# The gate z stored without its SiLU, squares summed by VectorE, and a norm placed between blocks of the first output product

## The chip, the cores and the metric

The kernel runs on one core of a Trainium2 chip. The metric is the time of one execution on the device in microseconds; the median of a few runs is compared. A profile shows one execution, instruction by instruction, on TensorE (PE, with its weight loads as PEld), VectorE (DVE), ScalarE (ACT), GpSimd (POOL) and SyncE (SP), whose queue issues most of the DMAs.

## The reference, cut to what matters

One layer of a decoder trunk with two parallel groups of heads, over 1056 tokens (1024 of a prompt, 32 of samples), width 1024:

```python
n = rmsnorm(h, g_in); z_a, xbc, dt_raw, z_b, u_b = split(n @ w_in)
# group A: SSD scan y over chunks of 128 tokens, then, in 2 groups of 512 channels,
y = y * silu(z_a)
ya = y * rsqrt(mean(y * y, -1) + EPS) * ssd_norm_g
# group B: S5 scan y, then the GLU
g = gelu(y)
yb = g * sigmoid(g @ glu_w + glu_b) * silu(z_b)
h = h + concat(ya, yb) @ w_out          # then a gate with a second norm, and the final norm
```

## The kernel before

All matrices are kept with channels on the 128 partitions and tokens along the free axis, in 8 tiles of 128 channels. Each product is made from three matmuls per step, since weights and operands are split into a high and a low part (`split`: ScalarE makes the high part, VectorE the low one). `dense` makes one output tile of 128 channels in three chunks of tokens, 24 matmuls to a chunk, into one of the three PSUM buffers `psd`, and calls `evac` for each chunk. Weights come through `take_w`, which loads and splits one tile ahead.

The order is planned: the program is written in one sequence, and a planner puts each engine's instructions in an order by a model of their times; an engine then runs its list strictly in that order, and so does the queue of SP. `behind(ins)` and `issue_after` force an instruction after another on the same engine.

The stages follow one another as here, in us of the profiled execution:

1. 0 to 210: the norm of the input, the tiles of u, and three tiles of `z_b`.
2. 210 to 476: convolution tiles, and between them 16 batches of the S5 scan (`s5_batch`, whose tables `mm`, `om`, `u8` are loaded into two buffers each, and which ends in the matmuls `yp`), sums of output weights (`wo_sums`), and five more tiles of `z_b`.
3. 476 to 657: 16 units of the SSD scan (`ssd_first`, `ssd_second`), eight tiles of `z_a` between them (by `z_tile`, as for `z_b`), and towards the end `g_tile`, which loads the S5 result and splits it for the GLU.
4. 657 to 742: the GLU. For each of 8 tiles m: 72 matmuls, and for each chunk of it the load of z_b (tile `gzl`), Tanh of the product (`zt`), the load of g (`gg`) and two scalar_tensor_tensor operations into `yb`; then `za_apply(m)`, which loads z_a (`zl`), multiplies it into `xs[m]`, squares the result and sums the squares of four tiles into `ysq`. All these small tiles share one pool `ev` of six buffers.
5. 742 to 912: the output product, seven block products `PROD` of eight blocks (24 matmuls each) with operands `opn` made by `operand`. `ya_norm(g)` normalizes a group of four tiles of `xs`: `rstd_tok` sums `ysq` over channels with 12 narrow matmuls into `nsp` and takes the root in small VectorE operations, `rstd_bcast` spreads it over partitions with 12 matmuls into `nrb`, and 12 scalar_tensor_tensor operations apply it. It is written for group 0 after tile 3 of the GLU and for group 1 after the GLU.
6. 912 to 1027: the gate, and the last norm.

In `z_evac` each chunk of z is made into 2·silu(z) before it is stored: ScalarE writes Tanh(z/2) and VectorE adds one and multiplies by z, from PSUM. The factors 0.25 and `4 * EPS` further on take the doubling back.

The profile names operations by the line of a helper: L77 is any ScalarE activation (`act`), L80 add, subtract and multiply, L92 scalar_tensor_tensor, L233 and L247 the matmuls of `dense` and `dense_k`, L1221 those of the output product, L274 and L296 those of the norm sums and their spreading, L309 and L312 those of the S5 batch. On SP's queue L743 and L754 store z, L767 loads `zl`, L1157 loads `gzl`, and L791 loads `mm`.

Of the kernel before, what the change touches and what calls it, by code (L numbers as in the profile page):

```python
# [10 lines left out]
AF = mybir.ActivationFunctionType  # L11
# [13 lines left out]
CW = 352  # L25
# [15 lines left out]
def hymba_ssd_s5_kernel(  # L41
# [216 lines left out]
    def rstd_tok(chunks, n, eps=EPS, after=None, pause=None):  # L258
# [6 lines left out]
        for c, sqs in enumerate(chunks):  # L265

            for i, q in enumerate(sqs):
# [4 lines left out]
                for j in range(gr):  # L272
# [4 lines left out]
                    if after is not None:  # L277
                        after = pe_end[0] = end
        v, y, t = (nw_p.tile([128, 16], F32, tag=q, name=q, bufs=b)[0:qt, 0:w]
                   for q, b in (("nv", 2), ("ny", 3), ("nt", 2)))  # L280
        ts(v, sp[0:qt, 0:w], 1.0 / n, eps, ALU.mult, ALU.add)
# [453 lines left out]
    def z_evac(j):  # L735
        dst = zb_d[j] if j < 8 else za_d[j - 8]

        def evac(c, t0, n, ps):
            t = ev("zt", n)
            if j >= 8:  # L740
                act(t, ps, AF.Tanh, scale=0.5)
                v_mid[0] = stt(t, t, 1.0, ps, ALU.add, ALU.mult)
                dma(out=dst[:, t0:t0 + n], in_=t)  # L743
                return

            nn = min(n, NPT - t0)
            for a, b, d0, ns in ((0, nn, 0, 8),) + (((nn, n, NPT, 4),) if nn < n else ()):
                v = t[:, a:b].rearrange("p (s c) -> p s c", s=ns)
                pv = ps[:, a:b].rearrange("p (c s) -> p s c", s=ns)
                act(v, pv, AF.Tanh, scale=0.5)  # L750
                v_mid[0] = stt(v, v, 1.0, pv, ALU.add, ALU.mult)
# [11 lines left out]
    def za_apply(j):  # L763
        for c in range(3):
            t0 = CW * c
            t = ev("zl")
            dma(out=t, in_=za_d[j, :, t0:t0 + CW])  # L767
            y = xs[j][:, t0:t0 + CW]
# [6 lines left out]
            else:  # L775
                act(t, y, AF.Square)
                add(ysq[c], ysq[c], t, G)
# [214 lines left out]

    def ya_norm(g):

        rt = rstd_tok([[ysq[c]] for c in range(3)], 512, 4 * EPS)
        for c in range(3):
            rs = rstd_bcast(rt[:, 4 * c:4 * c + 4])
            for i in range(4):
                y = xs[4 * g + i][:, CW * c:CW * c + CW]
                stt(y, y, vc[:, V_NG + 4 * g + i:V_NG + 4 * g + i + 1], rs, ALU.mult, ALU.mult)  # L1000
# [15 lines left out]
    k = 3  # L1016
# [134 lines left out]
    for m in range(8):  # L1151
# [3 lines left out]
        def evac(c, t0, n, ps):  # L1155
            z = ev("gzl", n)
            dma(out=z, in_=zb_d[m, :, t0:t0 + n])  # L1157
            t = ev("zt", n)
# [9 lines left out]
            for yv, a, b, s, s0 in ((y[:, 0:NPT], 0, nn, 8, t0 // 128),) + (((y[:, NPT:T], nn, n, 4, 0),) if nn < n else ()):  # L1168
                zv, tv = (r[:, a:b].rearrange("p (s c) -> p s c", c=128 if s == 8 else 8) for r in (z, t))
                stt(yv.rearrange("p (c s) -> p s c", s=s)[:, s0:s0 + zv.shape[1]], zv, 0.25, tv, ALU.mult, ALU.mult)  # L1170
# [14 lines left out]
    def banks():  # L1185
        return [f("psd")[:, 0:CQ] for f in (lambda n: psd_(), lambda n: psd_(), lambda n: psd_(), psa, psa, psb, psb, psb)]
# [253 lines left out]
```

## Time and profile before

| | |
|---|---|
| median of three runs | 1028.26 us (1025.12 to 1031.12) |
| the profiled execution | 1028.4 us |
| its span, first to last instruction | 1026.6 us |
| what lies around the span | 1.8 us |
| granted TensorE clock, mean | 0.994 of full speed |
| busy shares | PE 97%, DVE 79%, ACT 44%, POOL 16% |

A busy share is an average over six stages with different limits; matmuls are pipelined, so that PE counts as busy while one matmul is being fed and another drains. What PE is short of is its idle time, 1026.6 - 996.4 = 30.2 us over the whole span. A row of a stretch gives the busy time of each engine in it with the number of its instructions. A row of waits gives who waited, for whom, the sum in us, how often, and the longest.

### The profile page before, as it was taken

How to read it: one execution, taken by the hardware profiler on the slowest of the kernel's cores; microseconds unless marked ns; L12 is line 12 of the kernel's file. 1: busy time of each engine (PE TensorE's matmuls, PEld its weight loads, DVE VectorE, ACT ScalarE, POOL GpSimd, SP SyncE). 2: the span in 40 equal slices, each digit the busy share in tenths (PEclk: the TensorE clock that was granted, in tenths of full speed). 3: DMA queues.
4: the chain of work that ended last, by engine and by line, in shares of the span. 5: the costliest groups of instructions: out<-in, count | busy, mean ns of one | idle time of the engine just before them, and what ended most of it. 6: DMA issues, size and time to landing. Idle time of an engine off the chain costs nothing.

```text
span 1026.6 us, 19644 instructions
## 1 busy us (share of the span) xinstructions
PE 996.4 (97%) x7214; PEld 945.3 (92%) x7214; DVE 809.5 (79%) x1880; ACT 454.6 (44%) x1009; POOL 164.9 (16%) x183
## 2 busy tenths in 40 slices
PE   9999999999999989999999997999999999999997
PEld 8999999979899989899887886899999999999996
DVE  5889989675998978984687768868778879986466
ACT  5733223345453434354865436344345435464221
POOL 0000000000000000002144233121232015641221
PEclk9999999999999989999999999999999999999999
DMA  9633489774658687755366668675634323335123
GB/s 315 219 77 120 148 254 245 198 244 132 196 168 255 193 236 206 207 155 183 113 185 200 204 189 224 170 201 166 176 114 136 112 90 125 120 114 171 50 95 106
DMA packets 181072, 174.89 MB, mean 170 GB/s; under 512 B 47728, under 2 KB 145520, under 8 KB 180976
## 3 DMA queue, kind: packets, MB, share of 16 engines
q1 hardware_dynamic: 150944, 153.23, 50.1%
q10 hardware_dynamic: 30032, 20.40, 6.4%
q8 instruction: 57, 0.93, 0.4%
q14 instruction: 39, 0.32, 0.1%
HBM read 123.05 MB, written 54.73 MB: 173 GB/s over the span
## 4 chain that ended last, share of the span: by engine, by line
PE 54%; DVE 8%; DMA 6%; issue 4%; ACT 2%; SPq 1%; POOL 0%; POOLq 0%; DVEq 0%; ACTq 0%
PE psd L233 30%; PE psd L1221 15%; DMA mm<-md 2%; PE yp L312 2%; ACT ab L77 1%; DMA ab<-acs_d 1%; PE nrb L296 1%; PE yd L873 1%; DVE acc L92 1%; PE yo L922 1%; DMA gr<-gd 1%; PE st L925 1%; DVE x L92 1%; DVE sst L80 1%; PE nsp L274 1%
## 5 line engine op out<-in xcount | busy, mean ns | idle before, releaser
L233 PE MATMUL psd<-n_h,wl 128*128 128x352 f32 x840 | 274.3, 327 | 1.4 <-DVE wl L80 1.4
L233 PE MATMUL psd<-n_h,wh 128*128 128x352 f32 x840 | 274.8, 327 | 0.0
L233 PE MATMUL psd<-n_l,wh 128*128 128x352 f32 x840 | 274.5, 327 | 0.0
L1221 PE MATMUL psd<-opn,wh 128*128 128x264 f32 x896 | 164.6, 285 | 1.7 <-DVE opn L80 1.7
L233 PEld LDWEIGHTS psd<-n_h,wh 128*128 128x128 f32 x840 | 158.7, 189 | 6.4 <-issue 6.1
L233 PEld LDWEIGHTS psd<-n_h,wl 128*128 128x128 f32 x840 | 158.7, 189 | 5.6 <-issue 3.4
L233 PEld LDWEIGHTS psd<-n_l,wh 128*128 128x128 f32 x840 | 158.7, 189 | 3.2 <-issue 2.9
L1221 PEld LDWEIGHTS psd<-opn,wh 128*128 128x128 f32 x896 | 138.8, 188 | 2.1 <-DVE opn L80 2.1
L80 DVE TENSOR_TENSOR wl<-wr,wh 128x512 fp32r<-128x512 f32 x146 | 106.3, 755 | 39.4 <-ACT wh L77 34.1
L77 ACT ACTIVATE wh<-wr 128x512 fp32r<-128x512 f32 x147 | 85.4, 622 | 105.5 <-PE psd L233 64.9
L1221 PE MATMUL psd<-opn,wl 128*128 128x264 f32 x448 | 127.1, 284 | 0.0
L1221 PEld LDWEIGHTS psd<-opn,wl 128*128 128x128 f32 x448 | 84.3, 188 | 0.0
L77 ACT ACTIVATE ab<-ab,tok 128x128 f32<-128x128 f32 (+1 forms) x144 | 42.9, 379 | 51.7 <-DMA ab<-acs_d 37.0
L233 PE MATMUL psd<-g_h,wh 128*128 128x384 f32 (+1 forms) x168 | 54.4, 324 | 0.0
L233 PE MATMUL psd<-g_l,wh 128*128 128x384 f32 (+1 forms) x168 | 54.0, 321 | 0.0
L233 PE MATMUL psd<-g_h,wl 128*128 128x384 f32 (+1 forms) x168 | 53.9, 321 | 0.0
L233 PE MATMUL psd<-hg_h,gwh 128*128 128x400 f32 (+1 forms) x144 | 46.7, 324 | 0.0
L233 PE MATMUL psd<-hg_l,gwh 128*128 128x400 f32 (+1 forms) x144 | 46.4, 322 | 0.0
L233 PE MATMUL psd<-hg_h,gwl 128*128 128x400 f32 (+1 forms) x144 | 46.3, 322 | 0.0
L77 ACT ACT_TABLE_LOAD x27 | 34.6, 1283 | 25.0 <-DVE acc L92 12.6
L92 DVE SCALAR_TENSOR_TENSOR zt<-zt,psd 128x352 f32<-128x352 f32 (+2 forms) x56 | 25.9, 463 | 23.3 <-ACT zt L77 23.0
L80 POOL TENSOR_TENSOR xl<-xl,h 128x264 f32<-128x264 f32 x32 | 29.8, 936 | 84.1 <-DMA xl<-xT 34.9
(323 smaller groups left out, 2044.3 us busy)
## 6 DMA issues: line engine op xcount, KB each, us to landing
wr<-wall SPq DMA_DIRECT2D x128, 256.0 KB, 3.4
mm<-md SPq DMA_DIRECT2D x16, 512.0 KB, 5.9
wa<-wall SPq DMA_DIRECT2D x32, 256.0 KB, 4.5
ws_d<-wa SPq DMA_DIRECT2D x16, 512.0 KB, 5.1
ab<-acs_d SPq DMA_DIRECT2D x16, 512.0 KB, 5.0
wr<-ws_d SPq DMA_DIRECT2D x32, 256.0 KB, 2.8
ud<-ub ACTq DMA_DIRECT2D x8, 576.0 KB, 4.8
u<-ud SPq DMA_DIRECT2D x16, 288.0 KB, 5.0
```

The lines of the kernel that those rows point to most:

```text
L77: return S.activation(out=out, in_=in_, func=func, **kw)
L80: return (eng or V).tensor_tensor(out=out, in0=a, in1=b, op=op)
L92: return V.scalar_tensor_tensor(out=out, in0=a, scalar=s, in1=b, op0=op0, op1=op1)
L233: end = PE.matmul(out=ps, lhsT=a[:, ko + k, :], rhs=b, start=(i == 0), stop=(i == 3 * K - 1))
L274: end = PE.matmul(out=sp[0:qt, gr * c + j:gr * c + j + 1], lhsT=q[:, qt * j:qt * j + qt], rhs=ones[:, 0:1], start=(i == 0 and j == 0), sto ...
L296: end = PE.matmul(out=rb[:, qt * j:qt * j + qt], lhsT=y[:, j:j + 1].to_broadcast([qt, 128]), rhs=ident[0:qt, 0:qt], start=True, stop=True)
L312: self.last = f(*a, **kw)
L873: PE.matmul(out=yd[64 * (e % 2):64 * (e % 2) + 64, e // 2], lhsT=x1[:, e], rhs=mt[:, e], start=True, stop=True)
L922: PE.matmul(out=yo[:, i], lhsT=hg[:, 128 * i:128 * i + 128], rhs=ct[g][:, cols], start=True, stop=True)
L925: PE.matmul(out=st, lhsT=bk, rhs=x2.rearrange("p e q -> p (e q)"), start=True, stop=True)
L1221: PE.matmul(out=ps, lhsT=a[:, k, :], rhs=b, start=(k == 0 and q == 0), stop=(k == 7 and q == 2))
```

## The change

1. `z_evac` stores z itself: ScalarE copies each chunk from PSUM to `zt`, and VectorE has no part in it any more (56 scalar_tensor_tensor operations fall away). `v_mid`, the mark behind which `wo_sums` is forced, is then set by the convolution alone.
2. In the GLU stage ScalarE applies Silu to `gzl` (24 chunks) and to `zl` (24 chunks) in place, before they are used; the factor 0.25 becomes 0.5 and `4 * EPS` becomes `EPS`.
3. The sums into `ysq` (18 adds) go from GpSimd to VectorE.
4. `ya_norm(0)` moves from the end of GLU tile 3 to tile 4, ahead of `za_apply(4)`. The operands of the first block product are made in the other order: those of yb at tile 4, those of xs at tile 5. Those of the second block product likewise begin with yb.
5. `ya_norm(1)` is cut into pieces that stand between blocks of the first block product, and the matmuls of blocks 0 to 5 and of the pieces are forced into one order: after each of the blocks 0, 1 and 2 the four sums of one chunk, after block 2 the root, after block 4 the spreading and the 12 operations that apply it. Each block takes its PSUM buffer when it comes to it, and not all eight at the start.

```diff
             if j >= 8:
-                act(t, ps, AF.Tanh, scale=0.5)
-                v_mid[0] = stt(t, t, 1.0, ps, ALU.add, ALU.mult)
+                act(t, ps)
                 dma(out=dst[:, t0:t0 + n], in_=t)
...
-                act(v, pv, AF.Tanh, scale=0.5)
-                v_mid[0] = stt(v, v, 1.0, pv, ALU.add, ALU.mult)
+                act(v, ps[:, a:b].rearrange("p (c s) -> p s c", s=ns))
...
             dma(out=t, in_=za_d[j, :, t0:t0 + CW])
+            act(t, t, AF.Silu)
...
-                add(ysq[c], ysq[c], t, G)
+                add(ysq[c], ysq[c], t)
...
+    def ya_scale(g, c, rt):
+        rs = rstd_bcast(rt[:, 4 * c:4 * c + 4], pe_end[0])
+        for i in range(4):
+            y = xs[4 * g + i][:, CW * c:CW * c + CW]
+            stt(y, y, vc[:, V_NG + 4 * g + i:V_NG + 4 * g + i + 1], rs, ALU.mult, ALU.mult)
+
     def ya_norm(g):
-
-        rt = rstd_tok([[ysq[c]] for c in range(3)], 512, 4 * EPS)
+        pe_end[0] = None
+        rt = rstd_tok([[ysq[c]] for c in range(3)], 512)
         for c in range(3):
-            rs = rstd_bcast(rt[:, 4 * c:4 * c + 4])
...
+            ya_scale(g, c, rt)
...
             dma(out=z, in_=zb_d[m, :, t0:t0 + n])
+            act(z, z, AF.Silu)
...
+        if m == 4:
+            ya_norm(0)
         za_apply(m)
-        if m == 3:
-            ya_norm(0)
-        if m in (4, 5):
-            opn += operand("b11", range(4 * (m - 4), 4 * (m - 4) + 4))
-
-
-    ya_norm(1)
+        if m == 4:
+            opn = operand("b11", range(4, 8))
+        if m == 5:
+            opn = operand("b11", range(4)) + opn
...
+    def ya_piece(n):
+        if n < 3:
+            if n == 0:
+                ya1["sp"] = psa("nsp")
+            for j in range(4):
+                with behind(pe_end[0]):
+                    pe_end[0] = PE.matmul(out=ya1["sp"][0:88, 4 * n + j:4 * n + j + 1],
+                                          lhsT=ysq[n][:, 88 * j:88 * j + 88], rhs=ones[:, 0:1],
+                                          start=(j == 0), stop=(j == 3))
+        if n == 2:
+            ya1["rt"] = rstd_root(ya1["sp"][0:88, 0:12], 512)
+        if n == 4:
+            for c in range(3):
+                ya_scale(1, c, ya1["rt"])
...
-        bk = banks()
...
-                ps = bk[2 * i + c]
+                ps = bank(2 * i + c)
...
-                        PE.matmul(out=ps, lhsT=a[:, k, :], rhs=b, start=(k == 0 and q == 0),
-                                  stop=(k == 7 and q == 2))
+                        with behind(pe_end[0] if j == 0 and 0 < 2 * i + c < 6 else None):
+                            end = PE.matmul(out=ps, lhsT=a[:, k, :], rhs=b, start=(k == 0 and q == 0),
+                                            stop=(k == 7 and q == 2))
+                        if j == 0 and 2 * i + c < 6:
+                            pe_end[0] = end
+                if j == 0 and 2 * i + c < 5:
+                    ya_piece(2 * i + c)
...
-                    nxt += operand(PROD[j + 1][1], range(2 * i, 2 * i + 2))
+                    nxt += operand(PROD[j + 1][1], [(2 * i + q + (4 if j == 0 else 0)) % 8 for q in range(2)])
...
-        opn = nxt
+        opn = nxt[4:] + nxt[:4] if j == 0 else nxt
```

## Rows read from the trace of the kernel before

**Rows 1.** The page, part 1: busy time of each engine, share, instructions.

```profile
PE 996.4 (97%) x7214; PEld 945.3 (92%) x7214; DVE 809.5 (79%) x1880; ACT 454.6 (44%) x1009; POOL 164.9 (16%) x183
```

**Rows 2.** Stretches: length, busy us of each engine, clock, DMA share, GB/s.

```profile
657.40:742.30 84.90, 84.90 (x554) 84.90 (x553) 63.70 (x128) 31.99 (x65) 15.59 (x15) 1.00 0.66 187
...
617.00:657.00 40.00, 33.19 (x232) 26.52 (x230) 37.33 (x70) 20.46 (x46) 13.54 (x9) 0.96 0.72 196
210.00:476.00 266.00, 256.48 (x1872) 240.05 (x1871) 217.54 (x558) 118.84 (x257) 1.22 (x2) 0.99 0.67 197
```

**Rows 3.** What PE waited for, 210 to 476 us.

```profile
PE vi L309 <- DMA mm<-md: 6.5, 4, 2.9
PE vi L309 <- DVE tb L80: 1.2, 1, 1.2
```

**Rows 4.** The page, part 5: the group of z's VectorE operation.

```profile
L92 DVE SCALAR_TENSOR_TENSOR zt<-zt,psd 128x352 f32<-128x352 f32 (+2 forms) x56 | 25.9, 463 | 23.3 <-ACT zt L77 23.0
```

**Rows 5.** The chain that ended last, 252 to 276 us: start, us, what.

```profile
253.18 0.52 DVE zt L92
...
258.58 0.40 DVE zt L92
...
259.32 0.12 DVE zt L92
...
268.45 5.91 DMA mm<-md
...
274.40 0.33 PE vi L309
```

**Rows 6.** The same chain, 400 to 420 us.

```profile
415.44 0.43 DVE zt L92
```

**Rows 7.** What SP's queue waited for, whole span.

```profile
SPq L754 <- DVE zt L92: 32.8, 12, 12.9
...
SPq L743 <- DVE zt L92: 28.5, 10, 10.3
```

**Rows 8.** VectorE in order of time, at 617 us: start, us, operation, idle before.

```profile
617.10 0.52 DVE L92 SCALAR_TENSOR_TENSOR zt<-zt,psd 128x352 f32<-128x352 f32 x1 [4.48 <-ACT zt L77]
617.54 0.28 DVE L80 TENSOR_TENSOR yt<-yos,ee 128x128 f32<-128x128 f32 x1
...
619.30 0.73 DVE L92 SCALAR_TENSOR_TENSOR x<-x,dsk,yt 128x32 f32<-128x32 f32 x4
```

**Rows 9.** ScalarE in order of time: table loads, a Silu (128x1024) and a Tanh.

```profile
250.32 1.28 ACT L77 ACT_TABLE_LOAD   x1 [2.49 <-DMA acs_s<-dw]
251.62 1.18 ACT L77 ACTIVATE x<-acc 128x1024 f32<-128x1024 f32 x2
252.70 0.44 ACT L77 ACTIVATE zt<-psd 128x352 f32<-128x352 f32 x1
...
488.25 1.28 ACT L77 ACT_TABLE_LOAD   x1
```

**Rows 10.** Groups of the GLU stage, 657 to 742 us.

```profile
L92 DVE SCALAR_TENSOR_TENSOR yb<-gzl,gg 128x384 f32<-128x384 f32 (+2 forms) x29 | 18.7, 687 | 10.3 <-DMA gg<-gd 10.0
L80 POOL TENSOR_TENSOR ysq<-ysq,zl 128x352 f32<-128x352 f32 x15 | 15.6, 1063 | 68.0 <-ACT zl L77 68.0
...
L80 DVE TENSOR_TENSOR x<-zl,x 128x352 f32<-128x352 f32 x21 | 10.8, 544 | 3.0 <-DMA zl<-za_d 2.7
...
L77 ACT ACTIVATE zl<-x 128x352 f32<-128x352 f32 x15 | 7.3, 496 | 20.7 <-DVE x L80 19.8 <-DMA wr<-wall 0.8
```

**Rows 11.** The chain that ended last, 742 to 761 us.

```profile
742.34 7.69 PE psd L1221 x63
750.03 1.80 PE nsp L274 x24
751.83 5.60 PE psd L1221 x45
757.44 2.65 PE nrb L296 x24
```

**Rows 12.** SP's queue, GpSimd and VectorE in order of time, 742 to 765 us.

```profile
742.82 1.40 SPq L767 DMA_DIRECT2D zl<-za_d  x3
...
746.82 3.04 POOL L80 TENSOR_TENSOR ysq<-ysq,zl 128x352 f32<-128x352 f32 x3 [6.74 <-ACT zl L77]
...
758.34 5.99 DVE L92 SCALAR_TENSOR_TENSOR x<-x,vc,nrb 128x352 f32<-128x352 f32 x12 [0.43 <-PE nrb L296]
```

**Rows 13.** The tile zl: from issue to landing of its loads.

```profile
DMA to landing us min/median/max: 2.2/2.7/3.6
```

More of the change, by code (lines that the diff above doesn't have):

```diff
@@ L256, in rstd, with rstd_tok @@
         return rstd_bcast(rstd_tok([sqs], n))
-    def rstd_tok(chunks, n, eps=EPS, after=None, pause=None):
+    def rstd_tok(chunks, n, after=None, pause=None):
         sp = psa("nsp")
@@ L278, in rstd_tok, with rstd_root @@
                         after = pe_end[0] = end
+        return rstd_root(sp[0:qt, 0:w], n)
+    def rstd_root(sp, n):
+        qt, w = sp.shape
         v, y, t = (nw_p.tile([128, 16], F32, tag=q, name=q, bufs=b)[0:qt, 0:w]
                    for q, b in (("nv", 2), ("ny", 3), ("nt", 2)))
-        ts(v, sp[0:qt, 0:w], 1.0 / n, eps, ALU.mult, ALU.add)
+        ts(v, sp, 1.0 / n, EPS, ALU.mult, ALU.add)
         ts(y.bitcast(I32), v.bitcast(I32), 1, None, ALU.logical_shift_right)
@@ L748, in evac @@
                 v = t[:, a:b].rearrange("p (s c) -> p s c", s=ns)
-                pv = ps[:, a:b].rearrange("p (c s) -> p s c", s=ns)
-                act(v, pv, AF.Tanh, scale=0.5)
-                v_mid[0] = stt(v, v, 1.0, pv, ALU.add, ALU.mult)
+                act(v, ps[:, a:b].rearrange("p (c s) -> p s c", s=ns))
                 o = dst[:, 0:NPT] if d0 == 0 else dst[:, NPT:T]
@@ L990, in sample_end @@
             ssd_y(8, g, 32, yds[g], yo)
+    def ya_scale(g, c, rt):
[3 more added lines that the diff above has]
+            stt(y, y, vc[:, V_NG + 4 * g + i:V_NG + 4 * g + i + 1], rs, ALU.mult, ALU.mult)
     def ya_norm(g):
-        rt = rstd_tok([[ysq[c]] for c in range(3)], 512, 4 * EPS)
+        pe_end[0] = None
+        rt = rstd_tok([[ysq[c]] for c in range(3)], 512)
         for c in range(3):
-            rs = rstd_bcast(rt[:, 4 * c:4 * c + 4])
-            for i in range(4):
-                y = xs[4 * g + i][:, CW * c:CW * c + CW]
-                stt(y, y, vc[:, V_NG + 4 * g + i:V_NG + 4 * g + i + 1], rs, ALU.mult, ALU.mult)
+            ya_scale(g, c, rt)
     s5_es, sd_es = ExitStack(), ExitStack()
@@ L1169, in evac @@
                 zv, tv = (r[:, a:b].rearrange("p (s c) -> p s c", c=128 if s == 8 else 8) for r in (z, t))
-                stt(yv.rearrange("p (c s) -> p s c", s=s)[:, s0:s0 + zv.shape[1]], zv, 0.25, tv, ALU.mult, ALU.mult)
+                stt(yv.rearrange("p (c s) -> p s c", s=s)[:, s0:s0 + zv.shape[1]], zv, 0.5, tv, ALU.mult, ALU.mult)
         (dense_k if m == 0 else dense)(w, g_h, g_l, evac, chunks=PCH)
         yb.append(y)
+        if m == 4:
+            ya_norm(0)
         za_apply(m)
-        if m == 3:
-            ya_norm(0)
-        if m in (4, 5):
-            opn += operand("b11", range(4 * (m - 4), 4 * (m - 4) + 4))
-    ya_norm(1)
+        if m == 4:
+            opn = operand("b11", range(4, 8))
+        if m == 5:
+            opn = operand("b11", range(4)) + opn
     h_r = [row(f"h{m}") for m in range(8)]
@@ L1183, in hymba_ssd_s5_kernel, with bank @@
     hg_h, hg_l = [None] * 8, [None] * 8
-    def banks():
-        return [f("psd")[:, 0:CQ] for f in (lambda n: psd_(), lambda n: psd_(), lambda n: psd_(), psa, psa, psb, psb, psb)]
+    def bank(n):
+        return (psd_() if n < 3 else psa("psd") if n < 5 else psb("psd"))[:, 0:CQ]
+    ya1 = {}
+    def ya_piece(n):
[12 more added lines that the diff above has]
+                ya_scale(1, c, ya1["rt"])
     def hg_split(m):
```

## The prediction

> **What bounds the kernel now.** I read the page first, for the busy shares, then the busy times by stage, then what PE waited for in the stages with idle time, and only there the chain of waits back to its cause. The reader is to see in the page that PE is busy for 996.4 us [rows 1] of a span of 1026.6, so no change that leaves its matmuls as they are can win more than 30.2 us. In the stretches one sees where the idle time lies. In the GLU stage there is none: 84.90 busy of 84.90 [rows 2]. From 210 to 476 us it is 266.00 - 256.48 = 9.5 us, with VectorE busy for 217.54 (82%), and from 617 to 657 us it is 40.00 - 33.19 = 6.8 us, with VectorE busy for 37.33 of 40 [rows 2]. So the kernel is bound by PE, and VectorE is close behind it in two stretches, which are the only ones where freeing VectorE can matter. The rest of the idle time lies in the first 210 us and after the output product begins; nothing in the change reaches its causes there, and I count it as untouched.
>
> **The change part by part.** *VectorE's part in z goes.* 56 operations of 463 ns mean, 25.9 us in all, fall away [rows 4]; ScalarE's own operation stays, a copy in the place of a Tanh, over the same elements. Where VectorE is off the path that is worth nothing, and I look at the two stretches.
>
> From 210 to 476 us five tiles of z are made with four VectorE operations each, 20 × 0.463 = 9.3 us. PE's waits there that can hang on VectorE are five, 6.5 + 1.2 = 7.7 us, all at the first matmul of an S5 batch, four of them for the load of mm [rows 3]. I followed two back. Ahead of the load issued at 268.45 the chain passes through z's operation three times, 0.52 + 0.40 + 0.12 = 1.04 us [rows 5], since the store of a weight sum, and behind it in SP's queue the load of mm, waited for VectorE. Ahead of the one wait on VectorE itself it passes through 0.43 us [rows 6]. That is 1.47 us for two waits, and at that rate 3.7 us for five. The bounds: nothing, if planner or loads take the rest up, and 7.7 us, all the waits, since 9.3 us of VectorE's work goes. I take 3.7. What speaks for more is SP's queue: the stores of z stood in it waiting for VectorE for 32.8 + 28.5 = 61.3 us [rows 7], with loads queued behind them, and after the change they wait for ScalarE alone, some 0.5 us sooner each. I give that no price of its own, as most loads behind them are early enough; it is in the upper bound.
>
> From 617 to 657 us VectorE is nearly full. Just ahead of that, at 617.10, it stands idle for 4.48 us with z's operation at the head of its list, and that waits for ScalarE [rows 8]. Without it the operations behind it, on results that PE has already made (0.28 us and its like, and 0.73 us, 1.3 us together), can run in that gap, and z's own 0.43 us (from its start to that of the next) falls away there and once more at the last chunk of z: 1.3 + 2 × 0.43 = 2.2 us less in a stretch that VectorE fills [rows 8]. I take 2.0, a little off for the loads of the S5 result that share the path; bounds nothing and 6.8, the idle time there [rows 2].
>
> *Silu in the GLU stage.* 48 activations on 128x352 to 128x384. The trace has no Silu of that size; the nearest row is a Square of the same tile zl, 496 ns [rows 10]. So 48 × 0.50 = 24 us, on a ScalarE that is busy for 31.99 of 84.90 [rows 2]: 56 of 85, and PE hides it. The cover is PSUM: a chunk takes PE (84.9 - 4.5) / 21 = 3.8 us (norm matmuls taken off), and with three buffers its eviction may come two chunks, 7.7 us, late before PE waits. I take 0; the upper bound is in the rivals.
>
> Tanh and Silu alternate there, and a table load takes 1.28 us. The trace shows that it isn't needed between these two: after the load at 250.32 a Silu runs at 251.62 and a Tanh at 252.70 with none between [rows 9]. The last load stands at 488.25, for the exponentials of the SSD stage [rows 9]; so I expect one more load, or three if a Silu is planned between the last exponentials, 1.3 to 3.8 us on ScalarE, which is busy for 20.46 of 40 us there [rows 2]. I take 0.
>
> The Trainium skill (ScalarE: Activation LUTs, "Table sets: the hidden batching unit") says to batch activations by table set, and its list has Tanh with Exp and does not say where Silu is. By its "What ACT_TABLE_LOAD costs", 2.66 us for each switch with the drain, 48 switches would be an estimated 128 us. The trace has the same 1.28 us for the load, and no load between Silu and Tanh; so the rule stays a rival only.
>
> *Sums of squares.* 18 adds leave GpSimd, 15 of them in the stretch at 1063 ns, and come to VectorE at the 544 ns of a product of the same shape [rows 10]: 18 × 0.54 = 9.8 us on an engine busy for 63.70 of 84.90 [rows 2], thus 73.5 of 85. A buffer of `ev` is given back sooner, by 0.5 us for each add and by GpSimd's latency, which about pays for the Silu that holds it longer. Cost 0 while that cover stands.
>
> *Norm and operands moved.* Group 0's norm and the order of the operands move by one tile, three chunks of 3.8 us, within a stage where PE doesn't wait; the first product needs them a tile and a half later. Cost 0.
>
> *Group 1's norm between blocks.* PE's work is the same, 24 and 24 instructions, 1.80 and 2.65 us, and stands at nearly the same places: before, the sums came 7.69 us into the product and the spreading 15.1 us [rows 11]. What is new is that the order is forced and begins early. One block takes 24 × 7.69 / 63 = 2.93 us [rows 11], so the sums of chunk 0 stand at 742.34 + 2.93 = 745.3. The last z_a loads are issued from 742.82 [rows 12] and land 2.7 us later [rows 13], at 745.5; then Silu 0.50, product 0.54, Square 0.50, add 0.54: 747.6. PE waits 747.6 - 745.3 = 2.3 us, and all blocks of the product are queued behind it. Bounds: 0, if the loads get their buffers earlier than before; 4.6, if the sum is ready only when GpSimd's last was, at 746.82 + 3.04 = 749.9 [rows 12]. I take 2.3. Chunks 1 and 2 then have a block of time each. After block 4 three PSUM buffers hold the spread root, and block 5 needs the first of them: its four operations take 4 × 5.99 / 12 = 2.0 us [rows 12] after the first third of the spreading, 0.9 us, against the 2.65 us that PE spends on it [rows 11]: 0.3 us of wait, up to 1.6 if a weight split stands ahead on VectorE. I take 0.3. The second product's first operand needs nine of the twelve operations and a split, about 768 us, and PE comes to it at 742.34 + 8 × 2.93 + 4.45 + 2.6 = 772.8; nothing.
>
> **The sum.** -3.7 - 2.0 + 2.3 + 0.3 = -3.1 us. Against the profiled execution, 1028.4 (span 1026.6 and 1.8 around it), that is **1025.3 us**. The median of the runs, 1028.26, is the same within 0.2 us.
>
> **The rivals.** *All the stalls close.* The planner orders everything anew with 25.9 us less on VectorE; if the five waits go (7.7) and half the idle time at the end of the SSD stage (3.4), with no new wait in the product, it is 1028.4 - 11.1 = 1017.3 us. For it: VectorE is the releaser, direct or through SP, in the stalls that I followed. Against: four of the five end on a load.
>
> *Loads hide the gain.* If load time alone sets those waits, nothing is won, and the wait in the first product stays: 1028.4 + 2.6 = 1031.0 us. That is the case in which the change doesn't do what it removes work for.
>
> *The GLU falls behind (slower).* VectorE is idle there for 84.90 - 63.70 = 21.2 us, mostly waiting for loads into `ev` (10.0 for gg and 2.7 for zl among them [rows 10]). If these waits stayed as long as they are, with 9.8 us of adds on top and 0.50 us of Silu in the path of each of the 21 chunks, 10.5, VectorE would need 63.7 + 21.2 + 9.8 + 10.5 = 105.2 us for 84.9. PSUM hides 7.7, PE would wait 12.6: with the other terms 1025.3 + 12.6 = 1037.9 us. It decides from 84.9 + 7.7 - 73.5 = 19.1 us of waits on. For it: that is just less than the 21.2 of before. Against: a wait ends when its load lands, so adds before it shorten it, and buffers that GpSimd held are free sooner.
>
> *A table load at each change of function.* If Silu and Tanh needed tables of their own there, two loads in each of 24 chunks, 48 × 1.28 = 61.6 us, would bring ScalarE to 56 + 61.6 = 117.6 us in a stage of 84.9, 33 us more: 1058 us. That is the skill's batching rule at this kernel's own load time; the trace speaks against it [rows 9].
>
> **How the numbers follow.** Chances: the forecast 0.38, all stalls close 0.31, loads hide the gain 0.12, the GLU falls behind 0.15, table loads 0.04. 0.5% is about 5.1 us, which is about what a measurement here can tell from no change: below 1023.2 is faster, above 1033.5 slower. The forecast with the bounds of its terms runs from 1021 to 1029; I count 0.31 of it as the same and 0.07 as faster. So faster is 0.31 + 0.07 = 0.38, same 0.31 + 0.12 = 0.43, slower 0.19. The low end of the range, 1014, is where all the stalls close with the whole idle time of 617 to 657 (7.7 + 6.8 = 14.5 us off); the high end, 1036, takes in part of a GLU that falls behind and leaves the rest of it, and the table loads, out.
>
> **What the changed profile would show.** Right: no VectorE operation on zt before the GLU; PE's waits for mm down to about half of 6.5 us; PE still without idle time from the start to the end of the GLU, with ScalarE at some 56 of 85 us there and VectorE at some 73; one to three more table loads, none between Silu and Tanh; in the first product a wait of about 2 us at the first sums, on VectorE's add. Wrong: idle PE in the GLU at the first matmul of a chunk, waiting for Tanh, which itself waited behind a Silu for its load; or waits for mm as long as before. What would make the total wrong even if each part is right is the planner: with other times it may place S5 and SSD work otherwise, and the waits are set by that placing.

## The result, and the profile after

The changed kernel is slower: 1039.17 us median of 7 runs (1035.74 to 1044.55) beside 1029.17 for the kernel before (7 runs), a ratio of 1.010 with a 95% interval of 1.0071 to 1.013. The profiled execution took 1036.62 us, span 1034.8. The forecast was 1025.3 with a range to 1036, so even the high end was too low.

The page of the changed kernel, busy time of each engine and the group of table loads:

```profile
PE 995.8 (96%) x7214; PEld 944.9 (91%) x7214; DVE 794.9 (77%) x1842; ACT 480.2 (46%) x1062; POOL 147.8 (14%) x165
...
L77 ACT ACT_TABLE_LOAD x32 | 41.1, 1283 | 23.0 <-DVE acc L92 11.3
```

PE has the same 7214 matmuls and the same busy time as in [rows 1]; VectorE has 14.6 us less. PE's idle time grows from 30.2 to 39.0 us, which is more than the 8.2 us of the longer span. Where it lies, and where PE's matmuls run slower, is read from the stretches (length, busy us of PE, PEld, DVE, ACT, POOL, clock, DMA share, GB/s):

```profile
210.00:476.00 266.00, 260.20 (x1916) 243.12 (x1914) 212.47 (x541) 129.35 (x282) 5.04 (x14) 1.00 0.68 198
...
617.00:657.00 40.00, 35.04 (x230) 29.49 (x230) 38.79 (x66) 22.63 (x44) 11.18 (x9) 0.96 0.71 198
...
649.30:738.00 88.70, 87.24 (x547) 87.15 (x546) 64.63 (x135) 47.82 (x101) 0.00 (x0) 0.96 0.61 171
738.00:752.00 14.00, 4.91 (x39) 4.70 (x38) 10.61 (x21) 8.82 (x20) 1.21 (x1) 0.76 0.60 169
752.00:775.00 23.00, 22.55 (x179) 22.42 (x179) 13.60 (x33) 7.78 (x16) 4.37 (x6) 0.92 0.20 64
...
755.80:780.00 24.20, 23.75 (x202) 23.62 (x202) 16.48 (x37) 9.56 (x20) 6.53 (x5) 1.00 0.20 66
```

The first two answer to [rows 2]: PE is busy 3.7 us more from 210 to 476 us and 1.9 us more from 617 to 657. The GLU's tile 1 begins at 648.7 us instead of 656.8. But windows of fixed time no longer hold the same work (the planner has put PE's work in another order, and the last S5 matmul starts at 456.3 us instead of 475.2), and from 0 to 210 and 476 to 617 us PE is busy 1.6 and 2.0 us less. The same 4563 matmuls up to tile 1, before:

```profile
0.00:656.80 656.80, 635.59 (x4563) 585.86 (x4563) 528.43 (x1358) 302.50 (x719) 65.37 (x83) 0.99 0.65 193
```

and after:

```profile
0.00:648.70 648.70, 629.47 (x4563) 580.31 (x4563) 508.61 (x1302) 307.83 (x724) 63.59 (x83) 1.00 0.67 196
```

So PE's idle time up to tile 1 falls by only 2.0 us, from 21.2 to 19.2. The other 6.1 us of the 8.1 are the same matmuls in less busy time, with the granted clock at 1.00 instead of 0.99 on the mean.

Then the lead is lost. The GLU, which had PE busy for every microsecond at clock 1.00 [rows 2], has 1.5 us idle and a mean clock of 0.96. And from 738 to 752 us, at the head of the output product, PE works for 4.9 us of 14. From the first matmul of tile 1 to that of the product it is now 90.0 us (before 85.4), and the product's first eight blocks take 40.2 us (before 28.1): 8.1 us won, 4.6 + 12.1 = 16.7 lost.

What PE waited for in the changed kernel, longest group first (us in total, times, longest), and the place in order of time (start, us, operation, idle time before it):

```profile
PE nsp L1204 <- DVE ysq L80: 9.1, 1, 9.1
...
PE nsp L274 <- DVE ysq L80: 1.5, 1, 1.5
...
PE vi L313 <- DMA mm<-md: 0.7, 1, 0.7
```

```profile
741.47 0.28 PE L1246 MATMUL psd<-opn,wl 128*128 128x264 f32 x1
750.84 1.33 PE L1204 MATMUL nsp<-cs,ysq 128*88 128x1 f32 x8 [9.09 <-DVE ysq L80]
752.04 0.79 PE L1246 MATMUL psd<-opn,wh 128*128 128x264 f32 x2
752.63 0.42 PE L1246 MATMUL psd<-opn,wl 128*128 128x264 f32 x1
...
755.75 0.28 PE L1246 MATMUL psd<-opn,wl 128*128 128x264 f32 x1
```

One block is done, and PE stands 9.09 us at the first sums. Behind the wait a matmul of 128x264 takes 0.42 us instead of 0.28, until about 755.5.

In the GLU the 1.5 us of idle time are one wait too, at the sums of group 0:

```profile
697.82 1.33 PE L274 MATMUL nsp<-cs,ysq 128*88 128x1 f32 x8 [1.46 <-DVE ysq L80]
...
699.81 0.52 PE L233 MATMUL psd<-g_h,wl 128*128 128x384 f32 x1
...
704.47 0.33 PE L233 MATMUL psd<-g_h,wl 128*128 128x384 f32 x1
```

```profile
697.80:704.50 6.70, 6.68 (x26) 6.68 (x27) 6.63 (x16) 2.67 (x6) 0.00 (x0) 0.52 0.52 129
```

From 697.8 to 704.5 us the granted clock is 0.52 on the mean, nearly all at the lower of its two levels (1.2 of 2.4 GHz). The wait and about half of these 6.7 us are the 4.6 us that the GLU loses. No matmul of the GLU's tiles 1 to 7 waits for an eviction, here or in any other profile: their only idle time is at group 0's sums or their spreading, but for 0.04 us at most.

Why the sums were late is read from ScalarE and VectorE at the same place, in order of time:

```profile
744.49 0.44 ACT L77 ACTIVATE gzl<-gzl 128x288 f32<-128x288 f32 x1 [3.19 <-DMA gzl<-zb_d]
744.84 1.13 ACT L77 ACTIVATE wh<-wr 128x512 fp32r<-128x512 f32 x2
745.88 0.48 ACT L77 ACTIVATE zt<-psd,glb 128x288 f32<-128x288 f32 x1
746.26 0.48 ACT L77 ACTIVATE zl<-zl 128x352 f32<-128x352 f32 x1
```

```profile
742.93 2.10 SPq L768 DMA_DIRECT2D zl<-za_d  x3
```

```profile
749.40 0.96 DVE L80 TENSOR_TENSOR x<-zl,x 128x352 f32<-128x352 f32 x2
750.27 1.39 DVE L80 TENSOR_TENSOR ysq<-ysq,zl 128x352 f32<-128x352 f32 x3
```

ScalarE stood 3.19 us at the Silu of z_b's last chunk (gzl) for its load, with a weight split, the Tanh of a PSUM chunk that PE had ended at 738.8, and z_a's Silus (zl) behind it. The last z_a loads are issued 4.3 to 5.9 us into the product; before it was from 0.6 us on [rows 12]. From 650 to 742 us the loads of z_a stood in SP's queue, before and then in the changed kernel, for

```profile
SPq L767 <- DVE yb L92: 2.5, 5, 0.9
```

```profile
SPq L768 <- DVE gzl L92: 10.5, 5, 6.0
```

that is, mostly for buffers that VectorE's operations on z_b's chunks give back. So the adds end 13.0 us into the product instead of 7.7. The same is seen over the whole GLU in its groups (busy us, mean ns, then the idle time just before and what ended it):

```profile
L77 ACT ACTIVATE gzl<-gzl 128x384 f32<-128x384 f32 (+1 forms) x20 | 9.8, 492 | 14.0 <-DMA gzl<-zb_d 10.7 <-DVE opn L80 1.6 <-DVE yb L92 1.6
L80 DVE TENSOR_TENSOR x<-zl,x 128x352 f32<-128x352 f32 x19 | 9.5, 520 | 10.0 <-ACT zl L77 9.9
L77 ACT ACTIVATE zl<-zl 128x352 f32<-128x352 f32 x19 | 9.1, 497 | 15.1 <-DMA zl<-za_d 13.6 <-DVE yb L92 0.9 <-DVE wl L80 0.5
```

ScalarE stands 10.7 + 13.6 = 24.3 us for loads at the Silus, and VectorE's product, which waited 2.7 us for z_a's loads in [rows 10], waits 9.9 for the Silu.

### The profile page after: what moved, and what is told of

Its sections match the earlier page's. It is cut to its first block, busy times and chain, and to the rows that moved or that the text cites. A ratio compares the mean times of both kernels' runs of the same rounds, so it can differ in the third digit from the quotient of the medians.

```text
span 1034.8 us, 19616 instructions
## 1 busy us (share of the span) xinstructions
PE 995.8 (96%) x7214; PEld 944.9 (91%) x7214; DVE 794.9 (77%) x1842; ACT 480.2 (46%) x1062; POOL 147.8 (14%) x165
## 4 chain that ended last, share of the span: by engine, by line
PE 63%; DMA 14%; DVE 13%; ACT 4%; issue 4%; SPq 1%; POOL 0%; ACTq 0%; POOLq 0%; DVEq 0%
PE psd L233 38%; PE psd L1246 15%; DMA ab<-acs_d 2%; DMA wr<-wall 2%; ACT ab L77 2%; DVE x L92 2%; PE yp L316 2%; DMA gr<-gd 1%; DVE wl L80 1%; DMA mm<-md 1%; DMA gg<-gd 1%; DMA zl<-za_d 1%; DMA gzl<-zb_d 1%; DVE yb L92 1%; PE kp L316 1%
## 5 line engine op out<-in xcount | busy, mean ns | idle before, releaser
L80 DVE TENSOR_TENSOR wl<-wr,wh 128x512 fp32r<-128x512 f32 x146 | 102.2, 730 | 56.9 <-ACT wh L77 55.8
L80 POOL TENSOR_TENSOR xl<-xl,h 128x264 f32<-128x264 f32 x32 | 32.7, 1023 | 191.3 <-DVE ysq L80 102.4
L80 POOL TENSOR_TENSOR ssq<-ssq,xl 128x264 f32<-128x264 f32 x28 | 31.2, 1119 | 20.6 <-ACT xl L77 20.6
```

The source lines that it names most:

```text
L80: return (eng or V).tensor_tensor(out=out, in0=a, in1=b, op=op)
```

## The experiments

Two theories were set against each other. **A:** the forced place of group 1's sums does it, as PE's other blocks are queued behind them. **B:** the Silus in the GLU do it, by making the chain of loads, Silus and evictions late, wherever the sums stand. Each run's time is its ratio to the kernel before on the same chip. The other columns are read from the profiled execution, in order of time: the start of GLU tile 1, from there to the product ("GLU"), the product's first eight blocks ("product"), and how far into the product the last add of squares ended ("sums ready"). A ratio comes from its own comparison and need not be the quotient of two medians (those of e1, 1033.32 and 1028.42, would give 1.0048).

| run | ratio (95%) | tile 1 at | GLU | product | sums ready |
|---|---|---|---|---|---|
| before | 1 | 656.8 | 85.4 | 28.1 | 7.7 |
| after | 1.010 (1.0071–1.013) | 648.7 | 90.0 | 40.2 | 13.0 |
| e1_free | 1.0029 (1.0005–1.0053) | 652.2 | 88.9 | 34.9 | 16.7 |
| e2_pieces_alone | 1.0059 (1.0037–1.008) | 657.4 | 85.4 | 33.5 | 8.6 |
| e3_later | 1.007 (1.0049–1.009) | 656.2 | 90.9 | 34.2 | 15.4 |
| e4_apply_first | 1.0027 (1.0007–1.0047) | 653.9 | 88.5 | 29.0 | 1.2 |
| e5_silu_alone | 1.0062 (1.004–1.0084) | 652.0 | 91.7 | 32.3 | 10.9 |
| e8_square_own | 1.0125 (1.009–1.0159) | 659.7 | 91.3 | 38.5 | 12.3 |
| e12_silu_stored | 1.0262 (1.0229–1.0295) | 674.5 | 85.4 | 37.7 | 9.5 |
| e13_silu_stored_alone | 1.0194 (1.0162–1.0226) | 677.3 | 85.4 | 30.3 | 9.6 |
| e15_zb_silu_stored | 0.9977 (0.9954–1.0001) | 655.2 | 85.4 | 33.2 | 11.1 |
| e17_zb_stored_za_glu | 1.0062 (1.0037–1.0086) | 656.4 | 86.5 | 35.7 | 14.4 |
| e19_tanh_first | 1.0083 (1.0052–1.0115) | 652.3 | 86.5 | 38.7 | 11.8 |
| e22_adds_vector | 1.0017 (0.9996–1.0039) | 660.0 | 85.4 | 28.1 | 6.4 |
| e24_zb_stored_adds_vector | 0.9971 (0.9952–0.999) | 652.8 | 85.4 | 28.1 | 7.1 |
| e26_both | 1.0011 (0.9993–1.0028) | 657.4 | 88.6 | 28.7 | 1.2 |
| e27_zb_stored_za_first | 1.002 (0.9997–1.0043) | 652.2 | 94.6 | 26.2 | -5.8 |

In e27 group 1's sums and spreading (4.4 us of PE's work) lie in the GLU column. Tile 1's start scatters by several us between kernels whose PE lists are the same up to there (after, e1 and e3: 648.7, 652.2 and 656.2), so for the gain ahead of the GLU only means are used. A profile is of one execution: that of e8 is the longest of its 6 (1047.8 us for a median of 1040.5), that of e15 the longest of its 12 (1031.5 for 1026.2).

### The forced pieces: undone, alone, later

e1_free, from the changed kernel:

```diff
+    ya_norm(1)
...
-                        with behind(pe_end[0] if j == 0 and 0 < 2 * i + c < 6 else None):
...
-                if j == 0 and 2 * i + c < 5:
-                    ya_piece(2 * i + c)
```

> The changed kernel with its last part alone undone: group 1's norm stands whole behind the GLU again, and the product's blocks are free to go ahead of it. Theory A (the forced place of group 1's first sums lays bare that VectorE and ScalarE end the last z_a tile late): the wait of 9.1 us at the first sums and the slow block behind it (1.7 us) go, and PE runs blocks in the meantime; the 8.1 us won ahead of the GLU stay, less what the GLU's own slowness costs. 1025 to 1029 us, at or under the kernel before; the first product's eight blocks take 28 to 30 us again instead of 40. Theory B (the Silus in the GLU make its chain so late that any order waits): 1034 us or more, with PE's wait moved to another place of the product, or into the spreading of the root.

Measured: 1.0029, 1033.3 us. Undoing it takes off some 0.7%, but A's 1025 to 1029 isn't reached, and B's 1034 isn't either. The product still takes 6.8 us more than before, and PE waits there for Tanh and for the same sums, at the place that the planner gave them:

```profile
PE psd L1230 <- ACT zt L77: 2.2, 2, 1.2
PE nsp L274 <- DVE ysq L80: 1.4, 1, 1.4
```

e2_pieces_alone, from the kernel before (the pieces themselves as in the diff of the change, with `4 * EPS`, and the second product's operands in its order):

```diff
-    ya_norm(1)
+                if j == 0 and 2 * i + c < 5:
+                    ya_piece(2 * i + c)
```

> The kernel before with the last part alone: z stored with SiLU, adds on GpSimd, group 1's sums forced between the blocks of the first product, its first operand order as in the changed kernel. Theory A: the sums are ready 7.5 us into the product (GpSimd's last add), the first block ends after 2.9 us, so PE waits about 4.6 us and a block behind it may run at the lower clock, 0 to 1.7 us more: 1033 to 1036 us, slower than before by itself. Theory B: the forced order is harmless without the Silus in the GLU: 1027 to 1030 us.

Measured: 1.0059, 1035.2 us, as A had it. PE in order of time, and the stretch of the second block:

```profile
748.85 0.79 PE L1215 MATMUL nsp<-cs,ysq 128*88 128x1 f32 x8 [3.00 <-POOL ysq L80]
749.50 0.49 PE L1257 MATMUL psd<-opn,wh 128*128 128x264 f32 x2
...
750.68 0.64 PE L1257 MATMUL psd<-opn,wh 128*128 128x264 f32 x2
```

```profile
749.50:754.60 5.10, 5.10 (x34) 5.10 (x34) 2.41 (x2) 0.81 (x3) 3.01 (x3) 0.67 0.38 114
```

A wait of 3.00 us and a block with its sums at clock 0.67 make most of the 5.4 us. So both theories hold a part: the Silus without forced pieces (e1, with the other parts of the change) cost the product 6.8 us, the pieces without Silus 5.4, and the changed kernel, which has both, 12.1.

e3_later, from the changed kernel:

```diff
-                if j == 0 and 2 * i + c < 5:
-                    ya_piece(2 * i + c)
+                if j == 0:
+                    for n in {3: (0, 1, 2), 5: (4,)}.get(2 * i + c, ()):
+                        ya_piece(n)
```

> The changed kernel with the same forced pieces two blocks later: the three sums and the root behind the fourth block, the scaling behind the sixth. Theory A: the sums of the changed kernel were ready 12 us into the product, and the fourth block ends 11.7 us into it, so the wait of 9.1 us falls to about 1 us and the block behind it runs at full clock: 1028 to 1031 us. Theory B: the lateness shows again wherever the norm stands: 1036 us or more.

Measured: 1.007, 1036.3 us. The wait at the sums is down to 0.9 us as A said, and the product to 34.2, but the GLU in front of it takes 90.9, and PE now waits for evictions in the product, 1.0 and 1.1 us. The time is within B's 1036 us or more.

### Which Silu, and by what way

e5_silu_alone, from the kernel before (scales 0.25 and `4 * EPS` adapted):

```diff
-                act(t, ps, AF.Tanh, scale=0.5)
-                v_mid[0] = stt(t, t, 1.0, ps, ALU.add, ALU.mult)
+                act(t, ps)
...
+            act(t, t, AF.Silu)
...
+            act(z, z, AF.Silu)
```

> The kernel before with the move of SiLU alone: z stored as a copy, the Silus on ScalarE in the GLU stage; the adds of the squares stay on GpSimd, group 0's norm, the operands and group 1's norm stay where they were. Theory A (the forced place of the sums is what costs): 1021 to 1027 us, faster than before. Theory B (the Silus themselves make the GLU's chain of loads and evictions late, whatever the order; the runs with one part undone gave 1.003 of before without the forced pieces): the GLU takes 3 to 5 us longer than 85.4 and the first product 5 to 7 us longer than 28.05, which eats the 4 to 8 us won ahead of the GLU: 1029 to 1034 us.

Measured: 1.0062, 1034.4 us: B, and a little over it. Moving SiLU alone is already slower than before: 4.8 us won ahead of the GLU in its profile, 6.3 lost in the GLU and 4.2 in the product.

e8_square_own, from the changed kernel:

```diff
-                act(t, y, AF.Square)
-                add(ysq[c], ysq[c], t)
+                u = sq_p.tile([128, CW], F32, tag="sq", name="sq")
+                act(u, y, AF.Square)
+                add(ysq[c], ysq[c], u)
```

> The changed kernel, with the squares of z_a's chunks written to a buffer of their own instead of back into the chunk's buffer of the six in ev: that buffer is free after the product, two operations sooner. Theory B1 (the six buffers of ev are held longer because of the Silus, so the loads into them are issued late): the lag of the GLU shrinks by 1 to 2 us a tile, the wait at the first sums falls from 9.1 to 3 to 6 us and the time to 1031 to 1036 us. Theory B2 (ScalarE's own list, where each Silu stands in front of evictions and waits for its load, makes it late): no change, 1037 to 1041 us.

Measured: 1.0125, 1040.5 us. The wait at the first sums was 6.6 us, but nothing of that shows in the time. Giving z_a's buffers back two operations sooner is no help, so B1 is out for z_a's own buffers. The time is the one that B2 gave; the buffers of z_b's chunks, for which z_a's loads wait in the row above, were not tried.

e19_tanh_first, from the changed kernel:

```diff
-            act(z, z, AF.Silu)
             t = ev("zt", n)
-            act(t, ps, AF.Tanh, scale=0.5, bias=glb[:, m:m + 1])
+            th = act(t, ps, AF.Tanh, scale=0.5, bias=glb[:, m:m + 1])
+            with behind(th):
+                act(z, z, AF.Silu)
```

> The changed kernel with z_b's Silu forced behind the Tanh of the same chunk on ScalarE, so that no Tanh waits for that chunk's load. If ScalarE's place in line behind z_b's loads makes the GLU late: GLU 86 to 87 us instead of 90, the wait at the first sums 3 to 5 us instead of 9.1, 1030 to 1034 us. If the lateness comes through the buffers of ev and the bursts in which SP issues loads into them: no change, 1037 to 1041 us.

Measured: 1.0083, 1037.7 us. In the GLU it does what the first reading said; the stretch of tiles 1 to 7 has clock 1.00 again and under a microsecond of idle time:

```profile
652.30:738.80 86.50, 85.58 (x554) 85.06 (x553) 66.29 (x140) 49.74 (x106) 0.00 (x0) 1.00 0.66 181
```

The wait at group 0's sums is gone. That at group 1's hardly moves (8.0 us), and the time is the one of the second reading. So z_b's Silu in front of Tanh costs the GLU about 3.5 us, through group 0's sums, and group 1's sums are late by another way.

e17_zb_stored_za_glu, e5's kernel with z_b's Silu at the store:

```diff
-                act(v, pv)
+                act(v, pv, AF.Silu)
...
-            act(z, z, AF.Silu)
```

> The kernel before with z_b's SiLU at the store (as in the run above) and z_a's SiLU alone in the GLU stage: 24 Silus there instead of 48, none in front of a Tanh of the same chunk. If ScalarE's Silus of z_b, which stand between PSUM and its Tanh, make the GLU late: GLU 85 to 87 us, first product 28 to 30, 1023 to 1028 us. If z_a's Silus do it, which lengthen the chain to the sums: GLU 88 us or more, first product 32 or more, 1030 to 1034 us as with all the Silus.

Measured: 1.0062, 1034.3 us. The GLU takes 86.5 us as the first reading said, the product 35.7 as the second, and the sums are ready 14.4 us into it (PE waits 1.8 us for them there, and 2.0 for a weight split of VectorE). So each Silu has its own harm: z_b's makes most of the loss in the GLU, z_a's a loss in the product.

e4_apply_first, from the changed kernel:

```diff
+        za_apply(m)
         (dense_k if m == 0 else dense)(w, g_h, g_l, evac, chunks=PCH)
         yb.append(y)
-        za_apply(m)
```

(with `ya_norm(0)` ahead of it for m = 4)

> The changed kernel with z_a's tile written ahead of the GLU tile of the same number instead of behind it, so that its loads, Silus, products, squares and adds stand earlier in the lists of SP, ScalarE and VectorE; the forced pieces stay where they are. Theory A (what costs is that the last z_a tile comes last): the sums are ready before the product begins, no wait at the first sums: 1026 to 1030 us. Theory B (ScalarE and VectorE are behind in the GLU as a whole, since each Silu stands in line behind its load): the lateness moves to the GLU's own evictions, and PE waits there or for the second operand: 1034 us or more.

Measured: 1.0027, 1031.2 us. The work is the same and the pieces are as forced as ever, but the last z_a tile no longer comes last. Its adds end at 1.2 us into the product, PE takes the first sums without a wait, and the product is back at 29.0 us:

```profile
743.11 0.52 DVE L80 TENSOR_TENSOR ysq<-ysq,zl 128x352 f32<-128x352 f32 x1
```

```profile
745.30 0.72 PE L1204 MATMUL nsp<-cs,ysq 128*88 128x1 f32 x8
```

e26_both is this edit and that of e19 together.

> The changed kernel with both lateness causes undone: z_a's tile ahead of the GLU tile, and z_b's Silu behind the Tanh of its chunk on ScalarE; the forced pieces stay. If the two are the whole loss: GLU 86 to 87 us (4 less than in the changed kernel), first product 28 to 29, no wait at the first sums, 1024 to 1028 us. If something else of the change costs too: 1030 us or more.

Measured: 1.0011, 1029.4 us, between the two ranges, level with the kernel before and 0.9% under the changed one by the two ratios. The product is at 28.7; the GLU stays at 88.6 and not at 86 to 87. At group 0's sums, which stand ahead of GLU tile 4 here, a tile sooner than in the changed kernel, PE waits 1.7 us for VectorE's add, and the granted clock behind it is 0.55 from 696.7 to 700.2 us. So the two causes explain the loss in the product, and the some 3 us left in the GLU are that wait and the clock.

### Where else SiLU could go

e12_silu_stored and e13_silu_stored_alone apply one Silu at the store, straight from PSUM, and none in the GLU; e12 from the changed kernel, e13 from the one before:

```diff
-                act(t, ps, AF.Tanh, scale=0.5)
-                v_mid[0] = stt(t, t, 1.0, ps, ALU.add, ALU.mult)
+                act(t, ps, AF.Silu)
```

(the same for z_b's two pieces of a chunk; e12 has `act(t, ps)` there to begin with)

> The changed kernel without the Silus in the GLU: one Silu straight from PSUM, where z is stored, in the place of the copy, so that VectorE still has no part in z; adds on VectorE, norms and forced pieces as changed. Theory A and B together: the GLU takes 85 to 86 us again and the first product 32 to 35 us (the forced pieces' own share), while the gain ahead of the GLU stays: 1027 to 1032 us. If the forced order alone were the cost, the first product would take about 40 us as in the changed kernel and the time 1033 us or more.

> The kernel before with only this: one Silu on ScalarE where z is stored, straight from PSUM, in the place of Tanh and VectorE's operation. Nothing in the GLU or the product changes. If the 25.9 us taken off VectorE are worth what the changed kernel showed ahead of the GLU (0.6 to 8.1 us in three profiles of one order), this is faster than before: 1020 to 1026 us. If that gain was only the scatter of single profiles: 1026 to 1030 us.

Measured: 1.0262 and 1.0194, the two slowest of all. Neither theory had it. The table loads rose to 60, and ScalarE in order of time shows why:

```profile
L77 ACT ACT_TABLE_LOAD x60 | 77.0, 1283 | 24.0 <-PE yp L312 8.1
```

```profile
543.98 1.28 ACT L77 ACT_TABLE_LOAD   x1
545.27 1.06 ACT L77 ACTIVATE ab<-ab 128x1024 f32<-128x1024 f32 x1
546.35 1.28 ACT L77 ACT_TABLE_LOAD   x1
547.65 0.47 ACT L77 ACTIVATE zt<-psd 128x352 f32<-128x352 f32 x1
```

z_a's tiles are stored among the exponentials of the SSD stage (ab), and between Silu and Exp a table is loaded each way. Between Tanh and Exp none was, behind the last load at 488.25 [rows 9]; in the kernel before:

```profile
492.84 0.44 ACT L77 ACTIVATE zt<-psd 128x352 f32<-128x352 f32 x1
493.19 1.04 ACT L77 ACTIVATE ab<-ab 128x1024 f32<-128x1024 f32 x1
```

In e13 the GLU begins 20.5 us late. This is the rule on batching by table set (the Trainium skill, ScalarE: Activation LUTs, "Table sets: the hidden batching unit"), and here the trace agrees with it. With no Silu in the GLU, both have 85.4 us there; in e12 the forced sums still wait 5.6 us.

e15_zb_silu_stored makes that edit for z_b alone, whose last tile is stored ahead of the exponentials; z_a keeps Tanh and VectorE.

```diff
-                act(v, pv, AF.Tanh, scale=0.5)
-                v_mid[0] = stt(v, v, 1.0, pv, ALU.add, ALU.mult)
+                act(v, pv, AF.Silu)
```

> The kernel before with one edit: z_b's eight tiles, all stored before the SSD stage's exponentials, get their SiLU by one ScalarE Silu straight from PSUM in the place of Tanh and VectorE's operation; z_a's eight, which are stored among the exponentials, keep Tanh and VectorE. 32 of VectorE's 56 operations on z go, the GLU gets no Silu. If the gain ahead of the GLU is real and comes from VectorE's operations before 476 us: no more than one or two table loads more, GLU 85.4, first product 28, and 1021 to 1026 us. If the gain was scatter of single profiles: 1027 to 1030 us.

Measured: 0.9977, 1026.2 us. 32 table loads, five more where one or two were expected, and a GLU of 85.4. In the profile, that of the longest run, the product takes 33.2: GpSimd's adds ended 11.1 us into it, and PE waited 1.8 us in all for them, with the clock at 0.90 in that stretch. In the kernel before, the sums were ready at 7.7 us, just when PE came to them [rows 11]; nothing was in hand.

e22_adds_vector is the adds alone, on the kernel before:

```diff
-                add(ysq[c], ysq[c], t, G)
+                add(ysq[c], ysq[c], t)
```

> The kernel before with the adds of the squares on VectorE alone. The forecast costed this at nothing: 1026 to 1030 us. If VectorE's longer list delays the GLU (9.8 us more in 85): GLU 86 to 88 us, 1030 to 1033 us.

Measured: 1.0017, 1029.9 us, no difference that shows. PE is busy throughout the GLU and the eight blocks:

```profile
660.00:745.30 85.30, 85.30 (x554) 85.04 (x553) 68.56 (x145) 32.19 (x65) 0.00 (x0) 1.00 0.67 189
745.30:773.40 28.10, 28.10 (x242) 28.10 (x241) 23.46 (x50) 12.92 (x27) 5.35 (x6) 1.00 0.38 111
```

e24_zb_stored_adds_vector is e15 and e22 together.

> The kernel before with two edits: z_b's SiLU at the store by ScalarE alone, and the adds of the squares on VectorE, which ends the last of them 6.4 us into the product instead of 7.7 or 11.1. If the lateness of the last sums is what took the gain of the z_b edit alone (first product 33.2 us there), the first product falls to 28 to 29 us, the GLU stays at 85.4, and the time is 1021 to 1025 us, faster than both kernels. If the loads into ev make it late whoever adds: first product 31 us or more, 1025 to 1028 us.

Measured: 0.9971 (0.9952 to 0.999), 1025.6 us: faster than the kernel before by 0.3%, which its interval only just sets apart from nothing, and than the changed one by 1.3% by the two ratios. The time is 0.6 us above the first reading's range, the GLU and the product are as it said, and nothing is given back:

```profile
652.80:738.20 85.40, 85.40 (x554) 85.13 (x553) 68.89 (x145) 32.48 (x65) 0.00 (x0) 1.00 0.67 188
738.20:766.30 28.10, 28.10 (x243) 28.10 (x242) 24.00 (x51) 12.96 (x27) 5.36 (x6) 1.00 0.38 112
```

That the adds on VectorE helped z_b's edit is not shown: the ratios of e15 and e24, 0.9977 and 0.9971, differ by less than their intervals.

e27_zb_stored_za_first is e17 with the adds on VectorE and z_a's tile, with `ya_norm(0)`, ahead of the GLU tile.

> The kernel before with z_b's SiLU at the store, z_a's SiLU in the GLU (24 Silus), z_a's tile ahead of the GLU tile, and the adds on VectorE: all of VectorE's operations on z are gone and only the chain that is not in a hurry got longer. If lateness alone was the loss: GLU 85 to 87 us, first product 28 to 29, 1022 to 1026 us. If z_a's Silus cost wherever they stand, through the buffers of ev: GLU 88 us or more, 1028 us or more.

Measured: 1.002, 1032.1 us. The sums are early, but PE waits 3.1 us at group 0's, which now stand a tile sooner, and the GLU takes 90 us without group 1's norm. Being late has only changed its place.

## Why the prediction was wrong, point by point

**VectorE's part in z: the sign right, the size not shown.** The five waits of 7.7 us from 210 to 476 us [rows 3] became 2.1 (0.7 for mm, 1.4 for a weight split of VectorE), 5.6 us less where 3.7 was forecast, and from 617 to 657 us PE's idle time fell by 1.9 for 2.0. But the sum counted the rest as untouched, and it wasn't: idle time grew by 1.6 us from 0 to 210 us and by 2.0 from 476 to 617, so that up to tile 1 only 2.0 us went. What of this is VectorE's freed time and what the planner's new order isn't told apart. Over eight profiles with z stored as a copy (after, e1, e3, e4, e5, e8, e19, e26) tile 1 begins at 654.1 us on the mean, over three with z as before (before, e2, e22) at 658.1: 4.0 us won where 5.7 was forecast. The eight scatter from 648.7 to 659.7, which is too wide to tell the one from the other. The 8.1 us of the changed kernel's own profile is the most of the eight, and luck in part: 6.1 of it is no idle time.

**Silu in the GLU stage at 0: this step failed.** The parts of it were right: ScalarE was far from full (47.8 of 88.7 us), and no table is loaded between Silu and Tanh; of the five loads more (one to three were forecast), three stand at 619, 624 and 650 us, where the exponentials end. What was wrong is the cover. PSUM was to let an eviction come 7.7 us late before a matmul of the GLU waits, and none waited for one; the Tanh of the last chunk started 7.0 us late (745.88 for 738.8). But PE's sums of squares hang on the same lists of ScalarE, VectorE and SP, and they have no PSUM between: group 0's within the GLU, group 1's in the product, to which the lag was handed on. Measured: 4.6 us in the GLU, a wait of 1.5 at group 0's sums and the lower clock behind it, and (e1) 6.8 in the product, without any forced place. The sign of being wrong that the prediction gave, a chunk's first matmul waiting for Tanh, didn't come.

**Adds on VectorE at 0: right** (e22). The sums are even ready 1.3 us sooner in its profile, 6.4 for 7.7 us.

**Norm and operands moved at 0:** not tried alone. In the changed kernel group 0's sums wait 1.5 us, and the clock behind them falls, so the cost was not nothing there: "a stage where PE doesn't wait" held only while the sums came in time. But with Silu moved and the norm in its old place (e5) PE waits there as well, 2.8 us, and the GLU is no shorter.

**The wait at the first sums, +2.3 with a bound of 4.6: mis-sized.** It measured 9.1 us, and the block behind it 1.6 us more at the lower clock. Its working took the loads where they stood before, landed at 745.5, 3.2 us into the product, and ended 5.3 us into it; with the Silus the first add ends 12.1 us into it. The bound had the same flaw, since it was the old chain's end. Without Silus (e2) the wait was 3.0, near the 2.3 by luck, since GpSimd's adds and no Silu are in that chain; the lower clock behind it is a term that the sum didn't have. The bank wait behind the spreading was 0.5 for 0.3.

**The sum, with what was measured:** -4.0 (mean) or -8.1 (this profile) + 4.6 + 12.1 is +12.7 or +8.6, around the +10 of the medians. The rival "the GLU falls behind" (1037.9) had the sign and by chance nearly the number. Its mechanism, waits for loads that VectorE can't shorten, was nearly right too, but it put all 12.6 us into the GLU's own chunks, where none came (the 4.6 came at group 0's sums), and it stood on VectorE, while it was ScalarE that stood for the loads. That e19 mends the GLU and not the product shows the two ways apart. Why z_a's loads are issued 4 us later into the product stays open in part: SP's queue waits for buffers of z_b's chunks, e8 speaks against the time that z_a's chunks hold theirs, and a larger ring was not tried.

## What to carry to other kernels

An operation on an engine that is half idle isn't free if it must wait for a load: on an in-order engine everything behind it waits too, and slack in PSUM hides that only from the matmuls that write there. Before costing such a lag at nothing, look for the next instruction of PE that needs the end of the same chain, and ask how much is in hand there; here it was nothing (sums ready at 7.7 us, used at 7.69). And before an order is forced, measure when its operand is ready: with the same pieces the product took 12 us longer behind a late chain and 1 us longer behind an early one (e4).

## What the runs showed of the hardware

A short wait of PE can cost more than itself: behind 3.00 us of wait (e2) and 9.09 (after) the matmul of 128x264 went from 0.28 to 0.42 us for some 3 us, 1.4 and 1.6 us more over the block; behind 1.46 us in the GLU (after) the granted clock was 0.52 for 6.7 us. In e1 the matmul stayed at 0.28 behind 0.99 us (at 745.16) and went to 0.42 behind 1.37 us:

```profile
754.10 0.79 PE L274 MATMUL nsp<-cs,ysq 128*88 128x1 f32 x8 [1.37 <-DVE ysq L80]
...
755.14 0.42 PE L1230 MATMUL psd<-opn,wl 128*128 128x264 f32 x1
```

The length of the wait alone doesn't decide it. In e17 the matmul stayed at 0.28 behind 2.05 us:

```profile
751.18 0.39 PE L1220 MATMUL psd<-opn,wl 128*128 128x264 f32 x1 [2.05 <-DVE wl L80]
...
751.64 0.28 PE L1220 MATMUL psd<-opn,wl 128*128 128x264 f32 x1
```

The waits of e2, after and e1 behind which it slowed stood at the narrow sums (128x1), and those of 0.99 and 2.05 us between matmuls of 128x264. Narrow sums without a wait slowed nothing in the kernel before: its first eight blocks, with 24 of them [rows 11], take 28.1 us at clock 1.00. So at these places the clock fell where a wait and the narrow sums came together.

Silu and Exp don't share a loaded table, but Tanh ran next to either without a load. So Tanh with an extra operation of VectorE, among exponentials, was cheaper than one Silu: 27 loads against 60, and 20 us.
